# Moving GpSimd's two-input operations beside a gated recurrence to VectorE, in a hybrid decoder layer

## The chip, the core and the metric

The kernel runs on one core of one Trainium2 chip. The metric is the device time of one launch in microseconds (us), the median of the runs. The engines are named as in the profile: PE is TensorE (PEld its weight loads), DVE is VectorE, ACT is ScalarE, POOL is GpSimd, and SP is the queue that issues most transfers.

## What is computed

One layer of a decoder over 1024 positions of width 1024, in float32:

```python
proj = x @ w_in                      # [q | f | i | gate] of 4 x 512, attention q | k | v of 3 x 512
o_rec = hgrn2(q, f, i, gate)         # 4 heads of 128: S_t = diag(f_t) S_{t-1} + k_t^T i_t, o_t = S_t^T q_t
o_att = dilated_attention(aq, ak, av)  # 8 heads of 64, three window patterns
y = concat(o_rec, o_att) @ w_out
x = layer_norm(alpha * x + y)
x = layer_norm(alpha * x + relu(x @ w1)**2 @ w2)
```

In the recurrence q is silu(q), f = lb + (1 - lb) * sigmoid(f), k = 1 - f, and the output of each head is normalised, multiplied by a norm weight and by sigmoid(gate).

## The kernel before, in words

Products keep float32 accuracy by splitting an operand into a high part (a rounding copy on ACT) and a low part (raw minus high), and taking three matmuls: high*high, high*low and low*high.

The projection is cut into 22 weight tiles (`W_TILES`, lines 147 to 150). Fourteen of them (`NT1`) are run beside the recurrence: for each of two head groups v, two f, two q and g, then two tiles of attention v. The other eight (`LATE_TILES`) are run beside the attention. A tile is either natural (`natural_tile`, positions on the partitions, PSUM tile `nps`, eight steps of 24 matmuls) or transposed (`transposed_tile`, features on the partitions, PSUM tile `tps`, four steps of 24 matmuls). While tile n is computed, `w_conv` (line 170) splits the weights of tile n + 1 at step 2, and at step 4 if it has a second part: ACT copies the high part (L177), and POOL subtracts (L178). Tile 0 is split by DVE, in halves. Step 6 issues the load of tile n + 2 on SP. At the end of a g tile the sigmoid gates are multiplied by the norm weights, one 128x1024 product for each head, on POOL (L315).

The recurrence (`hgrn_group`, line 404) treats two heads at a time, as a tree over the sequence. `q` and `k` hold one head each as 128 features by 1024 positions; `tot` holds the decays. First the diagonal blocks are multiplied on PE (PSUM tile `lev`, 128 small matmuls), DVE keeps their diagonal (L424), and q is multiplied by the decay, head 0 on DVE and head 1 on POOL (L426). Then there are seven levels, j = 0 to 6. At each one PE computes the blocks between neighbouring segments of 2^j positions (`lev`), and DVE merges them into `dg` under a mask (L433, j under 5). Then each head's second half-segments of q are multiplied by the total decay of the first (DVE, L466), the first half-segments of k by the total decay of the second (POOL, L465), and the totals of the next level are formed (DVE, L468, into `totx`). Each L465 or L466 covers 128x512 elements, a strided half of the tile. The products of a level need the q and k of the level before. After level 4 the blocks of `dg` are copied to `AT` (L447 on ACT, L449 on DVE). Behind the last level k is transposed (`knps`, L482), states are built (`kvps`) and outputs formed (`ops`, normalised through a power on POOL, L526, and multiplied by the gates at L529).

The two streams are interleaved by `merge` (line 65): each stream states the cost of its steps, and the recurrence runs ahead until it has spent 0.7 of the projection's cost. That is the order in which the program is traced. Outside the first tile the framework's scheduler then fixes each engine's order at compile time; it prefers what was traced earlier among what it takes to be ready. On the chip every engine runs its own list strictly in order.

In the profile a line can be a helper's: all plain matmuls are L126, and the PSUM tile tells which they are. The k of the recurrence appears as `f` in POOL's rows, because both tiles of an f weight tile get that name.

Of the kernel before, what the change touches and what calls it, by code (L numbers as in the profile page):

```python
# [14 lines left out]
ALU = mybir.AluOpType  # L15
AX = mybir.AxisListType

P = 128
# [21 lines left out]
LATE_TILES = 8  # L40
# [49 lines left out]
def hybrid_layer_kernel(ctx: ExitStack, tc: tile.TileContext, x, w_in, w_out,  # L90
# [3 lines left out]
    PE, DVE, ACT, POOL, SP = nc.tensor, nc.vector, nc.scalar, nc.gpsimd, nc.sync  # L94
# [15 lines left out]
    def G(nm, dt=F32, shape=None):  # L110
        uid[0] += 1
        return gpool.tile(shape or [P, 1024], dt, name=f"{nm}_{uid[0]}", tag="g", bufs=50)
# [7 lines left out]
    def PS(tag, nm, shape=None):  # L120

        uid[0] += 1
        return ppool.tile(shape or [P, 512], F32, name=f"{nm}_{uid[0]}", tag=tag, bufs=PS_BUFS[tag])

    def mm(o, lhsT, rhs, start, stop, more=False):
        PE.matmul(o, lhsT, rhs, start=start, stop=stop, skip_group_check=more)  # L126

    def f32(ap):
        return ap.bitcast(F32)
# [17 lines left out]
    W_TILES = []  # L147
# [3 lines left out]
    W_COL = {"v": HI, "f": HF, "q": HQ, "g": HG, "av": AV, "aq": AQ, "ak": AK}  # L151
    NATURAL = ("v", "g", "av")
    wraw, whl = {}, {}

    def w_load(n, pieces=1):

        kind, g = W_TILES[n]
        nat = kind in NATURAL
        cw, kn = (256, 4) if nat else (128, 8)
        c0 = W_COL[kind] + cw * g  # L160
        wraw[n] = []
        for i in range(ND // kn):
            t = G("wraw", shape=[P, kn, cw])
            kp = kn // pieces
            for j in range(pieces):
                k0 = kn * i + kp * j
                SP.dma_start(t[:, kp * j:kp * (j + 1)], w_in[k0 * P:(k0 + kp) * P, c0:c0 + cw].rearrange("(k p) c -> p k c", p=P))
            wraw[n].append(t)

    def w_conv(n, i, engs=None):  # L170
        engs = engs or (POOL,)
        raw = wraw[n][i]
        hi, lo = G("whi", F32R, list(raw.shape)), G("wlo", F32R, list(raw.shape))
        kp = raw.shape[1] // len(engs)
        for j, eng in enumerate(engs):
            ks = slice(kp * j, kp * (j + 1))
            ACT.copy(hi[:, ks], raw[:, ks])  # L177
            eng.tensor_tensor(lo[:, ks], raw[:, ks], f32(hi[:, ks]), ALU.subtract)  # L178
        whl.setdefault(n, []).append((hi, lo))
# [10 lines left out]
    nrmw = cpool.tile([P, 512], F32, name="nrmw")  # L190
# [37 lines left out]
    def at_(tiles, kt, c0, n):  # L228
        return tiles[kt // 2][c0 // 512][:, kt % 2, c0 % 512:c0 % 512 + n]
# [41 lines left out]
    def natural_tile(n, kind, g, conv):  # L271

        if kind == "av":
            dst = [G("vs", F32R, [P, 8, P]) for _ in range(4)]
        else:
            dst = [G(kind, shape=[P, 8, P]) for _ in range(2)]
        for duo in range(4):
            ps = PS("s", "nps", [P, 2, 256])
            for i in range(2):
                sb = 2 * duo + i  # L280
                hooks = x_prep.get(sb, ()) if n == 0 else ()
                prods = [(kt, z, y) for kt in range(ND) for z, y in ((0, 0), (0, 1), (1, 0))]
                if n == 0 and sb == 0:
                    prods.sort(key=lambda v: v[2])
                for i_, (kt, z, y) in enumerate(prods):
                    if hooks and i_ % (24 // len(hooks)) == 0:
                        hooks[i_ * len(hooks) // 24]()
                    mm(ps[:, i, :], at_(xT["hl"[z]], kt, sb * P, P), whl[n][kt // 4][y][:, kt % 4, :],
                       i_ == 0, i_ == len(prods) - 1)
                conv(sb)  # L290
                yield 2600.0
            qs = slice(2 * duo, 2 * duo + 2)
            if kind == "av":
                for h in range(4):
                    i_ = ps[:, :, h * 64:(h + 1) * 64]
                    ACT.copy(dst[h][:, qs, 0:64], i_)
                    DVE.tensor_tensor(dst[h][:, qs, 64:128], i_, f32(dst[h][:, qs, 0:64]), ALU.subtract)
            else:
                for h in range(2):
                    i_ = ps[:, :, h * P:(h + 1) * P]  # L300
                    if kind == "g":
                        ACT.activation(dst[h][:, qs, :], i_, AF.Sigmoid)
                    else:
                        ACT.copy(dst[h][:, qs, :], i_)
        if kind == "av":
            if g == 0:
                at["v", 0], at["v", 1] = dst[0:2], dst[2:4]
            else:
                for h in range(4):
                    ACT.dma_start(v_d[h], f32(dst[h]).rearrange("p c v -> p (c v)"))  # L310
        else:
            for h in range(2):
                if kind == "g":
                    hh = 2 * g + h
                    POOL.tensor_tensor(dst[h], dst[h], nrmw[:, None, hh * P:(hh + 1) * P].to_broadcast([P, 8, P]), ALU.mult)  # L315
                    hd["gate", hh] = dst[h]
                else:
                    hd["v", 2 * g + h] = dst[h]
# [54 lines left out]
    def stage1_main(n0, n1):  # L373
# [4 lines left out]
        for n in range(n0, n1):  # L378
            kind, g = W_TILES[n]
            if n == 1:  # L380
                lower_bound()
            if n == NT1 - 2:
                SP.dma_start(bias, cf_d[:, C_BIAS:])
# [20 lines left out]
    def hgrn_group(g):  # L404
# [3 lines left out]
        q = [hd.pop(("q", h)) for h in heads]  # L408
        k = [hd.pop(("k", h)) for h in heads]
        tot = [hd.pop(("f", h)) for h in heads]  # L410
# [12 lines left out]
        blocks32(ps)  # L423
        DVE.tensor_tensor(dg, ps, dmask[:, None, :].to_broadcast([P, 16, 32]), ALU.mult)  # L424
        for i in range(2):
            (DVE if i == 0 else POOL).tensor_tensor(q[i], q[i], tot[i], ALU.mult)  # L426
        yield 3400.0
        for j in range(7):
            w = 1 << j
            if j < NLEV:  # L430
                ps = PS("t", "lev", [P, 16, 32])
                blocks32(ps)
                DVE.copy_predicated(dg, lmask[:, None, 32 * j:32 * j + 32].to_broadcast([P, 16, 32]), ps)  # L433
                cost = 3400.0
            elif j == 5:
                ps = PS("t", "lev", [P, 16, 32])
                for u in range(16):
                    kk, qq, c0 = k[u // 8], q[u // 8], (u % 8) * P
                    for b in (0, 64):
                        mm(ps[b:b + 32, u, :], kk[:, c0 + b:c0 + b + 32], qq[:, c0 + b + 32:c0 + b + 64], True, True)  # L440
                for i in range(2):
                    for b in (0, 64):
                        ACT.copy(AT[i][b:b + 32, :, b + 32:b + 64], ps[b:b + 32, 8 * i:8 * i + 8, :])
                    for b in range(4):
                        o = AT[i][32 * b:32 * b + 32, :, 32 * b:32 * b + 32]
                        if b % 2:
                            ACT.copy(o, dg[32 * b:32 * b + 32, 8 * i:8 * i + 8, :])  # L447
                        else:
                            DVE.tensor_copy(o, dg[32 * b:32 * b + 32, 8 * i:8 * i + 8, :])  # L449
                cost = 1800.0  # L450
            else:
                for i in range(2):
                    ps = PS("t", "lev", [64, 8, 64])
                    for c in range(8):
                        mm(ps[:, c, :], k[i][:, c * P:c * P + 64], q[i][:, c * P + 64:c * P + P], True, True)
                    ACT.copy(AT[i][0:64, :, 64:128], ps)
                cost = 1000.0

            n = S // (2 * w)
            for i in range(2):  # L460
                tv = tot[i].rearrange("p (n two) -> p n two", two=2) if j == 0 else \
                    totx[i][:, tofs:tofs + 2 * n].rearrange("p (n two) -> p n two", two=2)
                qv = q[i].rearrange("p (n two w) -> p n two w", two=2, w=w)[:, :, 1, :]
                kv = k[i].rearrange("p (n two w) -> p n two w", two=2, w=w)[:, :, 0, :]
                POOL.tensor_tensor(kv, kv, tv[:, :, 1:2].to_broadcast([P, n, w]), ALU.mult)  # L465
                DVE.tensor_tensor(qv, qv, tv[:, :, 0:1].to_broadcast([P, n, w]), ALU.mult)  # L466
                nofs = 0 if j == 0 else tofs + 2 * n
                DVE.tensor_tensor(totx[i][:, nofs:nofs + n], tv[:, :, 0], tv[:, :, 1], ALU.mult)  # L468
            tofs = 0 if j == 0 else tofs + 2 * n
            yield cost  # L470
# [63 lines left out]
        o_back(*pend)  # L534
        yield 450.0

    NT1 = len(W_TILES) - LATE_TILES
    bias, zt = G("bias"), G("zt", F32R, [P, 2, 2, 256])
    with tc.manual_schedule():
        for _ in stage1_main(0, 1):  # L540
            pass
    merge(stage1_main(1, NT1), flat(hgrn_group(0), hgrn_group(1)), R1)
    AT = None
# [212 lines left out]
    def filler():  # L756
        tail = stage1_main(NT1, len(W_TILES))

# [535 lines left out]
```

## Time and profile before

| what | value |
|---|---|
| median of three runs | 1264.65 us (1263.89 to 1265.03) |
| the profiled execution, its own time | 1261.03 us |
| its span, first to last instruction | 1259.2 us |
| PE busy | 1206.3 us (96%) |
| DVE busy | 809.8 us (64%) |
| ACT busy | 550.3 us (44%) |
| POOL busy | 303.7 us (24%) |
| mean granted TensorE clock | 0.991 |

A row of busy time counts how long an engine had an instruction in execution. Overlapping neighbours are pipelined, so that in the timeline the start of the next can lie before the end of the last. An instruction that waits for something while it is already counted as started is long in these rows. The granted clock is a share of the full 2.4 GHz; 0.5 is 1.2 GHz.

### The profile page before, as it was taken

How to read it: one execution, taken by the hardware profiler on the slowest of the kernel's cores; microseconds unless marked ns; L12 is line 12 of the kernel's file. 1: busy time of each engine (PE TensorE's matmuls, PEld its weight loads, DVE VectorE, ACT ScalarE, POOL GpSimd, SP SyncE). 2: the span in 40 equal slices, each digit the busy share in tenths (PEclk: the TensorE clock that was granted, in tenths of full speed). 3: DMA queues.
4: the chain of work that ended last, by engine and by line, in shares of the span. 5: the costliest groups of instructions: out<-in, count | busy, mean ns of one | idle time of the engine just before them, and what ended most of it. 6: DMA issues, size and time to landing. Idle time of an engine off the chain costs nothing.

```text
span 1259.2 us, 19842 instructions
## 1 busy us (share of the span) xinstructions
PE 1206.3 (96%) x7888; PEld 1024.8 (81%) x7888; DVE 809.8 (64%) x1302; ACT 550.3 (44%) x955; POOL 303.7 (24%) x231
## 2 busy tenths in 40 slices
PE   7998999899999989999999999999998999999996
PEld 7888988899787777887778888788886888888885
DVE  4035424562475664777796676766558798978788
ACT  5221342033576573654785554545555343334410
POOL 3236344633323333324200000000013132223100
PEclk9999999899999999999999999999999999999999
DMA  9000040003012576012215657566497636354312
GB/s 300 19 15 19 18 152 17 20 2 129 22 35 84 185 255 247 18 50 85 117 47 179 210 183 232 193 203 199 139 349 272 234 101 223 111 179 140 116 67 101
DMA packets 112765, 165.83 MB, mean 132 GB/s; under 512 B 8736, under 2 KB 64288, under 8 KB 112672
## 3 DMA queue, kind: packets, MB, share of 16 engines
q1 hardware_dynamic: 108400, 153.75, 36.3%
q10 hardware_dynamic: 4272, 10.82, 2.2%
q8 instruction: 62, 1.02, 0.3%
q14 instruction: 31, 0.25, 0.1%
HBM read 112.11 MB, written 52.43 MB: 131 GB/s over the span
## 4 chain that ended last, share of the span: by engine, by line
PE 77%; DVE 10%; DMA 4%; POOL 3%; issue 3%; ACT 3%; SPq 1%; DVEq 0%; POOLq 0%; ACTq 0%
PE f2ps L126 23%; PE tps L126 13%; PE nps L126 10%; PE fX L126 10%; PE pps L126 5%; PE fZ L126 5%; PE avps L126 3%; PE sps L126 2%; PE trps L630 2%; DVE tot L468 2%; PE fY L126 2%; DMA x<-x_d 2%; PE lev L126 1%; DVE w1l L817 1%; PE ops L126 1%
## 5 line engine op out<-in xcount | busy, mean ns | idle before, releaser
L817 POOL TENSOR_TENSOR h2l<-h2r,h2h 128x1024 fp32r<-128x1024 f32 x24 | 69.4, 2902 | 481.2 <-ACT h2h L816 444.3
L126 PE MATMUL f2ps<-w2l,h2h 128*128 128x512 f32 x448 | 174.5, 390 | 5.0 <-DVE w2l L817 5.0
L126 PE MATMUL f2ps<-w2h,h2l 128*128 128x512 f32 x448 | 174.0, 389 | 0.0
L126 PE MATMUL f2ps<-w2h,h2h 128*128 128x512 f32 x448 | 173.5, 389 | 0.5 <-ACT w2h L816 0.5
L126 PE MATMUL nps<-whi,xTh 128*128 128x256 f32 x384 | 113.9, 297 | 2.2 <-ACT whi L177 2.2
L126 PE MATMUL nps<-whi,xTl 128*128 128x256 f32 x384 | 110.2, 287 | 0.0
L126 PE MATMUL nps<-wlo,xTh 128*128 128x256 f32 x384 | 108.5, 285 | 0.0
L126 PEld LDWEIGHTS f2ps<-w2l,h2h 128*128 128x128 f32 x448 | 84.1, 188 | 23.8 <-DVE w2l L817 6.2
L126 PE MATMUL pps<-wo,oTs 128*128 128x512 f32 x384 | 100.8, 401 | 2.5 <-POOL wo L718 1.4
L126 PE MATMUL fX<-xh,w1h 128*128 128x512 f32 x256 | 100.0, 393 | 2.4 <-ACT hB L946 2.4
L126 PE MATMUL tps<-xTh,whi 128*128 128x512 f32 x256 | 101.8, 398 | 0.0
L126 PE MATMUL fX<-xl,w1h 128*128 128x512 f32 x256 | 100.0, 391 | 1.8 <-DVE xl L889 1.8
L126 PE MATMUL tps<-xTh,wlo 128*128 128x512 f32 x256 | 100.4, 392 | 0.0
L126 PE MATMUL tps<-xTl,whi 128*128 128x512 f32 x256 | 100.3, 392 | 0.0
L126 PE MATMUL fX<-xh,w1l 128*128 128x512 f32 x256 | 99.3, 390 | 0.0
L126 PEld LDWEIGHTS f2ps<-w2h,h2h 128*128 128x128 f32 x448 | 84.0, 188 | 18.2 <-ACT w2h L816 0.9
L126 PEld LDWEIGHTS f2ps<-w2h,h2l 128*128 128x128 f32 x448 | 84.1, 188 | 17.4
L1203 DVE TENSOR_TENSOR r<-r,f2ps 128x512 f32<-128x512 f32 x96 | 64.8, 680 | 30.1 <-PE f2ps L126 29.9
L126 PEld LDWEIGHTS pps<-wo,oTs 128*128 128x128 f32 x384 | 70.1, 190 | 17.4 <-POOL wo L718 2.9
L178 POOL TENSOR_TENSOR wlo<-wraw,whi 128x1024 fp32r<-128x1024 f32 x26 | 62.6, 2409 | 82.7 <-ACT whi L177 68.9
L612 POOL TENSOR_SCALAR pr<-pr,rec 128x896 f32<-128x896 f32 (+3 forms) x64 | 47.7, 748 | 140.4 <-DVE rec L611 119.9
L816 ACT CAST h2h<-h2r 128x1024 fp32r<-128x1024 f32 x56 | 58.8, 1050 | 44.3 <-PE f2ps L126 28.7
(205 smaller groups left out, 2733.7 us busy)
## 6 DMA issues: line engine op xcount, KB each, us to landing
h2r<-h_d SPq DMA_DIRECT2D x56, 512.0 KB, 4.8
w2r<-in_w_ff_dram SPq DMA_DIRECT2D x32, 512.0 KB, 5.8
wraw<-in_w_in_dram SPq DMA_DIRECT2D x26, 512.0 KB, 4.5
w1c<-in_w_ff_dram SPq DMA_DIRECT2D x32, 256.0 KB, 4.4
h_d<-hA SPq DMA_DIRECT2D x16, 512.0 KB, 3.7
h_d<-hC SPq DMA_DIRECT2D x16, 512.0 KB, 3.2
h_d<-hB SPq DMA_DIRECT2D x16, 512.0 KB, 4.4
att<-qk_d SPq DMA_DIRECT2D x12, 512.0 KB, 5.7
```

Of the source, the lines that this page charges most:

```text
L126: PE.matmul(o, lhsT, rhs, start=start, stop=stop, skip_group_check=more)
L178: eng.tensor_tensor(lo[:, ks], raw[:, ks], f32(hi[:, ks]), ALU.subtract)
L468: DVE.tensor_tensor(totx[i][:, nofs:nofs + n], tv[:, :, 0], tv[:, :, 1], ALU.mult)
L612: POOL.tensor_scalar(pr[:, 0:n], pr[:, 0:n], rec, 1.0, ALU.mult, ALU.mult)
L630: PE.transpose(ps[:, jj, tb, :], prs[tb][:, (j + jj) * P:(j + jj + 1) * P], ident)
L816: ACT.copy(hi, raw)
L817: eng.tensor_tensor(lo, raw, f32(hi), ALU.subtract)
L1203: DVE.tensor_tensor(rv, rv, ps, ALU.add)
```

## The change

The 18 low-part subtractions of weight tiles 1 to 13 (L178), the four gate products (L315), the first decay product of the second head (L426) and the 28 key decays (L465) are issued on DVE. At each level the key decay now stands behind the query decay of the same head and ahead of the totals. The subtractions of tile 14 and later stay on POOL, and so do the scaling of k (L344), the power of L526 and the memsets.

```diff
+    NT1 = len(W_TILES) - LATE_TILES
...
     def w_conv(n, i, engs=None):
-        engs = engs or (POOL,)
+        engs = engs or ((DVE,) if n < NT1 else (POOL,))
...
                 if kind == "g":
                     hh = 2 * g + h
-                    POOL.tensor_tensor(dst[h], dst[h], nrmw[:, None, hh * P:(hh + 1) * P].to_broadcast([P, 8, P]), ALU.mult)
+                    DVE.tensor_tensor(dst[h], dst[h], nrmw[:, None, hh * P:(hh + 1) * P].to_broadcast([P, 8, P]), ALU.mult)
...
         for i in range(2):
-            (DVE if i == 0 else POOL).tensor_tensor(q[i], q[i], tot[i], ALU.mult)
+            DVE.tensor_tensor(q[i], q[i], tot[i], ALU.mult)
...
-                POOL.tensor_tensor(kv, kv, tv[:, :, 1:2].to_broadcast([P, n, w]), ALU.mult)
                 DVE.tensor_tensor(qv, qv, tv[:, :, 0:1].to_broadcast([P, n, w]), ALU.mult)
+                DVE.tensor_tensor(kv, kv, tv[:, :, 1:2].to_broadcast([P, n, w]), ALU.mult)
```

## Rows read from the trace of the kernel before

**Rows 1.** The page's part 1: PE's busy time over the whole span.

```profile
PE 1206.3 (96%) x7888; PEld 1024.8 (81%) x7888; DVE 809.8 (64%) x1302; ACT 550.3 (44%) x955; POOL 303.7 (24%) x231
```

**Rows 2.** Stretches: us, busy time and count of each engine, PEclk, DMA share, GB/s.

```profile
82.00:155.00 73.00, 67.54 (x1310) 65.21 (x1309) 40.43 (x54) 15.03 (x34) 36.16 (x20) 0.98 0.06 17
155.00:205.00 50.00, 50.00 (x253) 42.15 (x252) 10.85 (x27) 17.56 (x52) 19.08 (x13) 1.00 0.33 106
205.00:310.00 105.00, 99.87 (x1568) 97.15 (x1567) 55.92 (x102) 29.02 (x94) 48.57 (x30) 0.97 0.10 32
```

**Rows 3.** PE's waits over the span: us in total, times, longest.

```profile
PE lev L126 <- DVE q L466: 7.3, 2, 3.6
...
PE knps L482 <- POOL f L465: 2.2, 4, 0.8
...
PE lev L126 <- POOL f L465: 0.7, 2, 0.4
```

**Rows 4.** Stretches around PE's two long waits, columns as in rows 2.

```profile
97.40:101.00 3.60, 0.05 (x1) 0.00 (x0) 3.60 (x11) 0.66 (x2) 1.88 (x1) 1.00 0.00 0
101.00:105.00 4.00, 3.79 (x138) 3.65 (x139) 3.41 (x5) 0.00 (x0) 2.68 (x2) 0.57 0.46 135
221.00:226.00 5.00, 1.52 (x97) 1.45 (x101) 4.93 (x13) 0.40 (x2) 2.84 (x3) 0.79 0.02 3
226.00:234.00 8.00, 8.00 (x95) 7.94 (x86) 2.61 (x3) 0.00 (x0) 2.58 (x2) 0.70 0.01 2
```

**Rows 5.** Timeline of DVE, 84 to 104 us: start, us, operation.

```profile
86.66 1.23 DVE L426 TENSOR_TENSOR q<-q,f 128x1024 f32<-128x1024 f32 x1 [2.24 <-PE lev L126]
...
88.41 2.90 DVE L468 TENSOR_TENSOR tot<-f 128x512 f32<-128x512 f32 x2
91.23 9.10 DVE L468 TENSOR_TENSOR tot<-tot 128x256 f32<-128x256 f32 x12
100.25 0.69 DVE L466 TENSOR_TENSOR q<-q,f 128x512 f32<-128x512 f32 x1
100.85 0.73 DVE L433 COPY_PREDICATED dg<-lmask,lev 128x512 f32<-128x512 int32 x1
```

**Rows 6.** Timeline of POOL, 84 to 104 us.

```profile
87.27 2.88 POOL L426 TENSOR_TENSOR q<-q,f 128x1024 f32<-128x1024 f32 x1 [5.61 <-PE lev L126]
91.09 1.61 POOL L465 TENSOR_TENSOR f<-f,f 128x512 f32<-128x512 f32 x1 [0.95 <-PE lev L126]
...
96.87 2.40 POOL L178 TENSOR_TENSOR wlo<-wraw,whi 128x1024 fp32r<-128x1024 f32 x1
```

**Rows 7.** Groups by form, 0 to 320 us: count, busy us, mean ns, idle before.

```profile
L178 POOL TENSOR_TENSOR wlo<-wraw,whi 128x1024 fp32r<-128x1024 f32 x20 | 48.2, 2412 | 56.4 <-ACT whi L177 42.6 <-issue 13.0 <-DVE q L466 0.6
L465 POOL TENSOR_TENSOR f<-f,tot 128x512 f32<-128x512 f32 x24 | 33.7, 1420 | 23.1 <-PE lev L126 23.0 <-POOL f L465 0.2
L466 DVE TENSOR_TENSOR q<-q,tot 128x512 f32<-128x512 f32 x24 | 30.4, 1272 | 27.6 <-PE lev L126 27.4
L468 DVE TENSOR_TENSOR tot<-tot 128x256 f32<-128x256 f32 x4 | 8.6, 2184 | 0.0
L466 DVE TENSOR_TENSOR q<-q,f 128x512 f32<-128x512 f32 x4 | 2.7, 682 | 0.0
L426 DVE TENSOR_TENSOR q<-q,f 128x1024 f32<-128x1024 f32 x2 | 2.5, 1225 | 4.5 <-PE lev L126 4.5
L468 DVE TENSOR_TENSOR tot<-tot 128x64 f32<-128x64 f32 x4 | 0.7, 214 | 0.0
```

**Rows 8.** Timeline of ACT, 84 to 104 us: the high parts of two weight pieces.

```profile
90.83 2.00 ACT L177 CAST whi<-wraw 128x1024 fp32r<-128x1024 f32 x2
```

**Rows 9.** The chain that ended last: PE's projection between two levels.

```profile
111.12 5.94 PE nps L126 x48
```

**Rows 10.** Timeline of PE near 456 us.

```profile
456.03 0.58 PE L126 MATMUL avps<-pth,vs 128*128 128x256 f32 x1 [2.14 <-DVE opair L688]
```

**Rows 11.** The stretch around that wait, columns as in rows 2.

```profile
455.00:460.00 5.00, 3.97 (x14) 3.47 (x15) 3.62 (x9) 3.46 (x7) 2.53 (x2) 0.66 0.79 313
```

More of the change, by code (lines that the diff above doesn't have):

```diff
@@ L535, in hgrn_group @@
         yield 450.0
-    NT1 = len(W_TILES) - LATE_TILES
     bias, zt = G("bias"), G("zt", F32R, [P, 2, 2, 256])
```

## The prediction
> **What bounds the kernel now.** The page's busy times come first: PE is busy 96% of the span, so only time in which PE idles or is clocked down can be won [rows 1]. The stretches then show where the change can act. In the two in which a head group's recurrence runs PE idles 5.5 us of 73 and 5.1 us of 105, and the granted clock is below 1; between them PE has no gap at all [rows 2]. PE's waits name the idle time: 7.3 us in two waits of the level products for a query decay on DVE, 0.7 us in two for a key decay on POOL, and 2.2 us in four, where the transposes of k wait for the last key decay on POOL [rows 3]. That is 10.2 of the 10.6 us. Last, the short stretches around the two long waits show what follows each: the clock falls to its lower level, 1.2 GHz, as PE comes back from an idle of 3.6 us. What this costs is the share of the clock withheld while PE worked: 4.00 x 0.43 = 1.7 us in the first group, and 1.52 x 0.5 + 8.00 x 0.30 = 3.2 us in the second, 4.9 us together [rows 4].
>
> Why was DVE late? Between 88.41 and 100.25 it ran nothing but the 14 products of the totals, ahead of the first query decay [rows 5]. They are not that long: the 128x64 form takes 0.21 us, but the 128x256 form 2.18 us, ten times as much for four times the data [rows 7]. Over those same microseconds POOL ran two-input operations almost without a pause: one of 2.88 us from 87.27, then four back to back until 99.27, where the last one, begun at 96.87, ends [rows 6]. DVE's next decay begins 1 us later. I read that as exclusion: a DVE operation with two SBUF inputs stands still while POOL has a two-input one in execution. The query decays carry the same mark: 0.682 us on average at level 0, 1.272 us at the other levels, for the same 128x512 [rows 7].
>
> **The parts, one by one.**
>
> *Key decays.* 28 operations leave POOL, where they took 1.42 us or more, and join DVE. The price on DVE is that of the query decay of the same shape and stride, 0.68 us, and DVE's next operation starts 0.60 behind such a one (100.25, 100.85) [rows 5, 7]. A plain level is then four decays and one masked copy, 5 x 0.61 = 3.1 us, in the cover of 48 projection matmuls of 5.94 us [rows 9]. If that cover were gone, 3.1 us would lie on the path at each of 14 levels.
>
> *Weight low parts, gate products, first decay of head 1.* 18 + 4 + 2 operations of 128x1024 at DVE's 1.225 us in place of 2.41 us for the low parts [rows 7]: 2 x 1.2 of them in the first two levels of a group, two gate products in one later level, one or two low parts in another. Such a level costs 3.1 + 2.5 = 5.6 us at most, still under 5.94, with little to spare. Low parts outside the recurrence lie beside stretches in which DVE is busy 10.85 of 50 us [rows 2], and cost nothing. The SP loads issued behind them wait for the same buffers, free a little earlier.
>
> *The first level, which decides.* From 86.66 DVE runs two first decays, 2.45 us, and the diagonal, 0.6: 89.7. The totals without a blocker are, for each head, 0.68 (the price of 128x512), about 0.42 and 0.28 (estimates between 0.68 and 0.21 by size), 0.21, and three shorter ones of about 0.17, 2.1 us in all: two heads end at 93.9. Then head 0's two decays to 95.1; one low part to 96.3, whose high part is ready from 91.8 [rows 8]; the masked copy to 96.9; head 1's decays to 98.1. PE comes free at 97.4, needs head 0 first and head 1 some 0.65 us later, at 98.1. So the wait falls from 3.6 us to nothing, or to 1.2 if both low parts are queued ahead of head 1. Bounds for each group: 0 (best order) and 3.6 (as now); more only if the long forms are DVE's own price, a rival below. I take 0.3, nearest to the order in which POOL's own rows place the two low parts around a decay [rows 6].
>
> *Waits that shrink a little.* The 0.7 us behind POOL's key decays goes, since no 2.4 us operation of POOL stands ahead of them. Of the 2.2 us before the transposes I let 0.3 us go: two serial decays of 0.6 take the place of one of 1.42.
>
> *Waits that are added.* Behind a low part on DVE's strictly ordered list stand the decays of a level, and for those waits PE. If its high part is late, all wait. Bounds: 0, as all covers above suffice, and 0.3 + 2.45 us at each of the levels with three 1.2 us operations. I take 1.1 us over both groups. What is late next is DVE itself in the level with the gates.
>
> *The clock.* No idle of 3.6 us, no fall: 4.9 us back. How short a gap must be for that, the trace doesn't say sharply: near 456 us a wait of 2.14 us was also followed by a stretch at 0.66 [rows 10, 11], while the waits of up to 0.8 us in rows 3 were not.
>
> *The sum.* 7.3 - 0.6 = 6.7, plus 4.9, 0.7 and 0.3, less 1.1: 11.5 us. Against the profiled execution's own 1261.03 that gives 1249.5. That execution stands 3.6 us below the median of the runs, and I take the same difference for the changed kernel: 1264.65 - 11.5 = 1253.2 us. Beyond 310 us nothing is changed, and PE is the bound, so an earlier start should carry through to the end.
>
> **The rivals.**
>
> *Half of it.* DVE's list may put both low parts, or the totals of later levels, between level 0's products and head 1's decays. A wait of 2.3 us then stays in each group, and the clock still falls, as it did behind 2.14 us [rows 10, 11]. The gain is 2 x 1.3 + 0.7 + 0.3 = 3.6 us: 1261.0. For it: the low parts do fall just there [rows 6]. Against: the totals alone give back more than 7 us.
>
> *Absorbed.* The first 310 us end earlier, but the attention's order or its transfers give it back: 1264 us, within 0.2% of before. For it: a scheduler that sees other engine loads may order later work otherwise. Against: nothing in that part waits for a fixed point in time.
>
> *Slower: DVE is the bound by itself.* The long rows could be DVE's own price for strided and short accesses, and not POOL's doing. Then a level costs 4 x 1.27 + 0.61 = 5.7 us, a low part in it makes 6.9 (1.0 over the cover), two gate products 8.2 (2.2 over): about 4.2 a group. The totals keep their 11.8 us and the first wait grows by the decay, the key decays and the low part that now precede, some 2.5 us. Together 2 x 6.7 = 13.4 us: about 1278. It decides from 5.94 us a level on. Against: level 0's decays, stride two as well, take 0.682 [rows 7].
>
> The spacing itself is shown: 0.60 us from the start of an operation of 0.69 to the next [rows 5]. The Trainium skill (VectorE: DVE Perf Modes, sections "The DRAIN you can't avoid" and "Rules for kernel authors") speaks against this change: behind each operation it puts a flush of about the duration less 266 ns, unless the next one may start earlier, and asks for few operations. By that flush a plain level would cost about 5.6 us, one with a low part 7.8 and one with two gates 10, the first wait would be about 6.6, and the sum would be an estimated 18 us slower than before; the trace shows no such gap, so it gets no chance beyond this rival's.
>
> **How the numbers follow.** The forecast has 0.75, half of it 0.13, absorbed 0.07, slower 0.05. The forecast's own range is 1249.5 (all 10.2 us and the 4.9 back) to 1258. The range reaches up to the half case, 1261, and leaves out the other two. A measurement of this kernel can tell about 0.2%, 2.5 us, from no change: the half case is still faster by that. So faster 0.86, same 0.08, slower 0.06.
>
> **What would show it right or wrong.** Right: DVE's totals of 128x256 near 0.4 us and its decays near 0.7; PE's wait for L466 under 1 us each; granted clock 1.00 from 82 to 310; that stretch shorter by about 11 us, and all behind it unchanged. Wrong: the long forms stay long with POOL idle (exclusion is not the cause); or they shrink and PE still waits, now for DVE behind a low part or a gate; or the stretch shrinks and the attention grows.

## The result and the profile after

The changed kernel takes 1249.29 us (median of five runs, 1248.10 to 1250.61) against 1263.89 us for the kernel before on the same chip (1261.03 to 1265.03): a ratio of 0.989, 95% interval 0.9878 to 0.9903, 14.6 us faster. Between the two profiled executions it is 12.9 us, 1261.03 to 1248.10.

The stretches of the changed kernel, with the columns of [rows 2] and [rows 4]:

```profile
82.00:155.00 73.00, 73.00 (x1352) 70.25 (x1351) 39.75 (x80) 18.37 (x52) 1.68 (x2) 1.00 0.06 17
205.00:310.00 105.00, 105.00 (x1467) 100.60 (x1467) 53.17 (x128) 35.15 (x105) 12.82 (x9) 1.00 0.15 52
97.40:101.00 3.60, 3.60 (x148) 3.43 (x147) 3.53 (x14) 0.66 (x2) 0.00 (x0) 1.00 0.02 5
101.00:105.00 4.00, 4.00 (x35) 3.94 (x33) 0.79 (x2) 0.00 (x0) 0.00 (x0) 1.00 0.02 4
```

PE has no gap left beside the recurrence and works at the full clock throughout; none of the three waits of [rows 3] exists any more. The last high-part projection matmul of tile `nps` begins at 294.1 us instead of 309.3. So 15.2 us were won there, and the next stage, the attention, starts earlier by the same 15.2 (first `sps` at 319.0 instead of 334.2). The high-part matmuls of `nps`, before and after (count, shortest, median and longest in ns, first and last start in us):

```profile
L126 PE MATMUL nps<-whi,xTh x384: 277/283/583, 8.3 to 309.3; 128*128 128x256 f32 x192
```

```profile
L126 PE MATMUL nps<-whi,xTh x384: 277/283/582, 8.3 to 294.1; 128*128 128x256 f32 x192
```

The groups of DVE between 0 and 320 us, by form (L466, L467, L469, L179 and L450 are L466, L465, L468, L178 and L449 before):

```profile
L179 DVE TENSOR_TENSOR wlo<-wraw,whi 128x1024 fp32r<-128x1024 f32 x18 | 21.7, 1222 | 7.1 <-ACT whi L178 7.1
L466 DVE TENSOR_TENSOR q<-q,tot 128x512 f32<-128x512 f32 x24 | 16.4, 684 | 14.4 <-PE lev L126 14.2
L467 DVE TENSOR_TENSOR f<-f,tot 128x512 f32<-128x512 f32 x24 | 16.4, 683 | 0.0
...
L467 DVE TENSOR_TENSOR f<-f,f 128x512 f32<-128x512 f32 x4 | 2.7, 684 | 0.0
...
L450 DVE COPY AT<-dg 32x256 f32<-32x256 f32 x8 | 2.2, 280 | 0.1
L469 DVE TENSOR_TENSOR tot<-tot 128x256 f32<-128x256 f32 x4 | 1.5, 424 | 0.0
```

Against [rows 7] the query decays fall from 1.272 to 0.684 us and the 128x256 totals from 2.184 to 0.424. DVE has 52 instructions more, but its busy time in the two stretches falls slightly, from 96.3 to 92.9 us [rows 2], though the second stretch now ends 15 us further into what follows. Over the whole span it rises by 6.0 us, to 815.8; at 0.684 us for a decay and 1.222 for a 128x1024 operation the 52 would add an estimated 48.

The timeline of DVE around the first level, start and duration in us:

```profile
88.89 1.22 DVE L427 TENSOR_TENSOR q<-q,f 128x1024 f32<-128x1024 f32 x1
90.02 1.29 DVE L469 TENSOR_TENSOR tot<-f 128x512 f32<-128x512 f32 x2
91.23 0.97 DVE L469 TENSOR_TENSOR tot<-tot 128x256 f32<-128x256 f32 x3
92.11 0.68 DVE L466 TENSOR_TENSOR q<-q,f 128x512 f32<-128x512 f32 x1
...
94.54 0.68 DVE L467 TENSOR_TENSOR f<-f,f 128x512 f32<-128x512 f32 x1
95.14 2.35 DVE L179 TENSOR_TENSOR wlo<-wraw,whi 128x1024 fp32r<-128x1024 f32 x2
97.41 1.19 DVE L469 TENSOR_TENSOR tot<-tot 128x128 f32<-128x128 f32 x9
```

Two things differ from [rows 5], not one. No operation is long, and **DVE's list has another order**: only 5 of the 14 totals stand ahead of the decays of level 0; the other 9 have moved behind them. Nobody wrote that into the change. It is the compile-time scheduler's answer to the change, and the experiments had to tell the two apart.

### The profile page after: what moved, and what is told of

The parts are those of the page before. It is cut to its first block, busy times and chain, and to the rows that moved or that the text cites. A ratio compares the mean times of both kernels' runs of the same rounds, so it can differ in the third digit from the quotient of the medians.

```text
span 1246.3 us, 19786 instructions
## 1 busy us (share of the span) xinstructions
PE 1203.6 (97%) x7888; PEld 1022.3 (82%) x7888; DVE 815.8 (65%) x1354; ACT 550.3 (44%) x955; POOL 204.9 (16%) x179
## 4 chain that ended last, share of the span: by engine, by line
PE 81%; DVE 7%; DMA 4%; ACT 3%; issue 3%; POOL 2%; SPq 1%; DVEq 0%; POOLq 0%; ACTq 0%
PE f2ps L126 23%; PE tps L126 13%; PE nps L126 11%; PE fX L126 10%; PE pps L126 5%; PE fZ L126 5%; PE avps L126 3%; PE sps L126 2%; PE trps L630 2%; DMA x<-x_d 2%; PE fY L126 2%; PE lev L126 2%; PE ops L126 1%; DVE w1l L817 1%; DMA qk_d<-ak 1%
## 5 line engine op out<-in xcount | busy, mean ns | idle before, releaser
L126 PEld LDWEIGHTS nps<-whi,xTh 128*128 128x128 f32 x384 | 74.6, 194 | 3.2 <-ACT whi L178 2.4
L126 PEld LDWEIGHTS nps<-whi,xTl 128*128 128x128 f32 x384 | 74.5, 194 | 0.0
```

## The experiments

The table gives medians, ratios to the kernel before on the same chip, and PE's idle time in the stretches 82 to 155 and 205 to 310 us together (10.6 us before, from [rows 2]). In all of these kernels the granted clock of both stretches is 1.00.

| kernel | us | ratio, 95% interval | PE idle, us |
|---|---|---|---|
| changed kernel | 1249.29 | 0.989 (0.9878 to 0.9903) | 0 |
| decays only | 1250.80 | 0.9911 (0.9892 to 0.993) | 2.7 |
| low parts and gates only | 1251.31 | 0.9906 (0.9889 to 0.9923) | 4.5 |
| changed, spare two-input work | 1251.24 | 0.9913 (0.9892 to 0.9933) | 2.5 |
| changed, spare memsets | 1250.05 | 0.9886 (0.9859 to 0.9914) | 0 |
| 4 low parts only | 1254.53 | 0.9927 (0.9908 to 0.9945) | 5.0 |
| 2 first decays only | 1252.37 | 0.9916 (0.989 to 0.9941) | 3.6 |
| before, totals behind | 1251.28 | 0.9915 (0.99 to 0.9931) | 3.0 |
| changed, totals ahead | 1249.96 | 0.9897 (0.9882 to 0.9911) | 0 |

### Does GpSimd's work hold VectorE, wanted or not?

Three kernels add work to GpSimd that nobody reads. All other engines' lists are those of the changed kernel. Spare two-input products:

```diff
+    scr = cpool.tile([P, 384], F32, name="scr")
+    def spare(h):
+        for c in (0, 320, 640):
+            POOL.tensor_tensor(scr, h[:, c:c + 384], h[:, c:c + 384], ALU.mult)
...
+        if 0 < n < NT1:
+            spare(f32(hi).rearrange("p k c -> p (k c)"))
```

> The changed kernel, and beside each low part of tiles 1 to 13 GpSimd also computes three two-input products of 128x384 from the high part into a scratch tile that nothing reads, as soon as the high part is there. The lists of all other engines are the same. Theory (holding): VectorE's totals, decays and copies in these stretches grow to over 1 us on average though they wait for no result, PE's waits before level 1 come back with 1.5 to 4 us in each group: 1254 to 1262 us. Rival (late results of GpSimd): nobody waits for GpSimd, so the time is that of the changed kernel, 1249 to 1250 us.

In the second kernel a copy of one element per partition and three memsets stand in place of the products:

```diff
...
+        POOL.tensor_copy(scr[:, 0:1], h[:, 0:1])
...
+            POOL.memset(scr, 0.0)
...
```

> As the kernel with spare products, but in place of each three products stand a copy of one element a partition (it makes GpSimd start at the same time) and three memsets of 128x384, which read no SBUF. Theory (holding by operations that read two inputs): VectorE's operations stay at their prices, 0.68 us for 128x512, 1249 to 1251 us. If any activity of GpSimd that writes SBUF holds VectorE: operations beside it grow by up to 1 us and the time goes to 1251 to 1255 us. Rival (late results): 1249 to 1250 us.

In the third, a scaling:

```diff
...
+            POOL.tensor_scalar(scr, h[:, c:c + 384], 1.0, 1.0, ALU.mult, ALU.mult)
...
```

> As the kernel with spare two-input products, but with one-input operations (a scaling) of 128x384. Theory (GpSimd holds VectorE for as long as it reads SBUF, with one input as well): VectorE's totals and low parts beside them grow, by less than with two inputs, since each lasts about half as long: 128x1024 low parts between 1.25 and 1.45 us on average. Rival (two inputs are needed): all of VectorE's operations keep their prices, as beside memsets.

The groups by form, 0 to 320 us, with the two-input products:

```profile
L185 DVE TENSOR_TENSOR wlo<-wraw,whi 128x1024 fp32r<-128x1024 f32 x18 | 26.1, 1463 | 7.1 <-ACT whi L184 7.1
...
L475 DVE TENSOR_TENSOR f<-f,f 128x512 f32<-128x512 f32 x4 | 4.0, 1002 | 0.0
...
L477 DVE TENSOR_TENSOR tot<-tot 128x128 f32<-128x128 f32 x4 | 2.4, 599 | 0.0
...
L175 POOL TENSOR_TENSOR scr<-whi 128x384 f32<-128x384 f32 x54 | 65.3, 1209 | 108.1 <-ACT whi L184 105.1
```

With the memsets:

```profile
L186 DVE TENSOR_TENSOR wlo<-wraw,whi 128x1024 fp32r<-128x1024 f32 x18 | 21.9, 1231 | 7.0 <-ACT whi L185 7.0
...
L476 DVE TENSOR_TENSOR f<-f,f 128x512 f32<-128x512 f32 x4 | 2.8, 694 | 0.0
...
L176 POOL MEMSET scr<- 128x384 f32 x54 | 22.8, 423 | 3.1
L174 POOL COPY scr<-whi 128x1 f32<-128x1 f32 x18 | 21.5, 1194 | 116.0 <-ACT whi L185 115.8
```

The memsets do run beside decays, as the timelines of POOL and of DVE show:

```profile
93.57 1.38 POOL L176 MEMSET scr<- 128x384 f32 x3
```

```profile
94.00 0.69 DVE L475 TENSOR_TENSOR q<-q,f 128x512 f32<-128x512 f32 x1
94.60 0.69 DVE L476 TENSOR_TENSOR f<-f,f 128x512 f32<-128x512 f32 x1
```

With the scalings:

```profile
L185 DVE TENSOR_TENSOR wlo<-wraw,whi 128x1024 fp32r<-128x1024 f32 x18 | 23.6, 1322 | 7.0 <-ACT whi L184 7.0
...
L475 DVE TENSOR_TENSOR f<-f,f 128x512 f32<-128x512 f32 x4 | 3.3, 834 | 0.0
...
L175 POOL TENSOR_SCALAR scr<-whi 128x384 f32<-128x384 f32 x54 | 47.8, 884 | 118.5 <-ACT whi L184 115.2
```

Work of which nobody awaits a result stretches DVE's low parts from 1.222 to 1.463 us and the first key decays from 0.684 to 1.002. Scalings do it too (1.322 and 0.834), memsets don't (1.231 and 0.694). The kernel with scalings was run once, 1249.07 us. So the holding is real, and of the three kinds of spare work only the two that read SBUF hold. It is mutual: the copy of one element per partition takes GpSimd 1.19 us beside DVE's low parts. But the time was forecast too high: with the products PE's waits came back with 2.5 us in all, 1251.24 us, with an interval that overlaps that of the changed kernel. None of them stands before level 1, where they were expected: 1.7 us lie at later levels of the second group, 0.8 before its transposes. By the time alone, theory and rival aren't told apart here; the rows of DVE do that. Holding VectorE need not cost PE anything.

The Trainium skill (SBUF — State Buffer, section "SBUF: two separate sides") says that the two engines share one pair of ports under an exclusive lock, held for a whole instruction, and that a VectorE operation with two SBUF inputs contends only with GpSimd operations that read SBUF. The rows above agree on what holds: 1.002 and 0.834 beside reading work, 0.694 beside memsets. That a hold lasts a whole instruction is not read from them.

### Which part of the change was needed?

Decays on VectorE, the rest back on GpSimd:

```diff
-        engs = engs or ((DVE,) if n < NT1 else (POOL,))
+        engs = engs or (POOL,)
...
-                    DVE.tensor_tensor(dst[h], dst[h], nrmw[...], ALU.mult)
+                    POOL.tensor_tensor(dst[h], dst[h], nrmw[...], ALU.mult)
```

> Only the decays (28 key decays and the first decay of head 1) are on VectorE; the 18 low parts and four gate products are back on GpSimd. PE's order is that of the changed kernel, instruction for instruction. Theory (a two-input operation of GpSimd holds VectorE's operations on SBUF): the two low parts of 2.4 us that fall beside level 0 stop VectorE from about 92 to 97 us, so a wait of 1 to 3 us comes back before level 1 in each group, perhaps with a fall of the clock: about 1255 us, 1251 to 1259; 128x512 decays again above 0.8 us on average. Rival (what cost time was that the key decays came late from a slow engine, whoever ran beside): all key decays are as fast as in the changed kernel, no wait, 1249 to 1250 us.

The timelines of DVE and of POOL around level 0:

```profile
93.59 2.28 DVE L466 TENSOR_TENSOR q<-q,f 128x512 f32<-128x512 f32 x1
95.80 2.89 DVE L467 TENSOR_TENSOR f<-f,f 128x512 f32<-128x512 f32 x1
98.61 1.20 DVE L469 TENSOR_TENSOR tot<-tot 128x128 f32<-128x128 f32 x9
```

```profile
92.15 5.99 POOL L179 TENSOR_TENSOR wlo<-wraw,whi 128x1024 fp32r<-128x1024 f32 x2 [10.35 <-ACT whi L178]
```

The two low parts hold head 1's decays as expected, 2.28 and 2.89 us in place of 0.68. But PE waited only 0.5 us for them, since head 0's decays were through and 9 totals stood behind. 1250.8 us instead of the 1255 expected: the time lies between the theory's range and the rival's, and it is the long rows that speak for holding.

The reverse, low parts and gates on VectorE, the key decays and the first decay of head 1 back on GpSimd:

```diff
-            DVE.tensor_tensor(q[i], q[i], tot[i], ALU.mult)
+            (DVE if i == 0 else POOL).tensor_tensor(q[i], q[i], tot[i], ALU.mult)
...
-                DVE.tensor_tensor(kv, kv, tv[:, :, 1:2].to_broadcast([P, n, w]), ALU.mult)
+                POOL.tensor_tensor(kv, kv, tv[:, :, 1:2].to_broadcast([P, n, w]), ALU.mult)
```

> Only the low parts and the gate products are on VectorE; the key decays and the first decay of head 1 are back on GpSimd. Theory (holding): the first decay of 2.9 us and the key decays of level 0 still stop the totals, some 4 to 5 us of holding beside level 0 in place of 11: a wait of 0.5 to 2 us before level 1, and the four waits before the transposes of k back with about 2 us: 1253 us, 1250 to 1257. Rival (late key decays): nearly the whole difference to the kernel before stays, 1259 to 1264 us.

PE's waits, 30 to 310 us (us in total, times, longest):

```profile
PE knps L483 <- POOL f L467: 2.6, 4, 0.8
PE lev L126 <- DVE q L466: 1.8, 2, 0.9
```

1251.31 us: the key decays on the slow engine are not what cost the time. Here all 14 totals still stand ahead of the decays, and 0.9 us of wait is left in each group. Either half of the change gives most of the whole, so the parts don't add up. The next two kernels start from the kernel before and move very little.

Four of the 52 operations, the low parts that fall beside level 0 and 1:

```diff
-        engs = engs or (POOL,)
+        engs = engs or ((DVE,) if n in (6, 12) else (POOL,))
```

> The kernel before with only 4 of the 52 operations moved to VectorE: the low parts of the two weight tiles (6 and 12) that are split beside levels 0 and 1 of each group. PE's order is that of the kernel before. Theory (GpSimd holds VectorE, and it costs time only where the held work outlasts PE's projection beside it, which is the case before level 1 alone): without these 4.8 us of holding in each group the wait before level 1 falls from 3.6 to about 1 us, the clock doesn't fall, and some 9 to 11 of the 13 to 15 us come back: 1251 to 1255 us. The waits before the transposes of k stay at about 2 us. Rival (each held operation costs its share, so 4 of 52 give little): a wait over 2.5 us stays, 1257 to 1263 us.

Two of the 52, the first decays of head 1:

```diff
-            (DVE if i == 0 else POOL).tensor_tensor(q[i], q[i], tot[i], ALU.mult)
+            DVE.tensor_tensor(q[i], q[i], tot[i], ALU.mult)
```

> The kernel before with only 2 of the 52 operations moved: the first decay of the second head, once in each group. Theory (holding, and the totals as what is held): from 91 to 99 us GpSimd's key decays and low parts still follow each other without a pause, so the totals finish where they did, the wait before level 1 stays at 2.5 to 3.7 us and the clock falls: 1259 to 1264 us. Rival (the first operation of the chain sets all behind it): the wait shrinks by the 1.6 us that this decay gets faster, to 2 us, and the clock may hold: 1253 to 1259 us.

Four low parts: 1254.53 us, and the wait before level 1 falls to 0.9 us in each group, as expected; all 14 totals still stand ahead. Two first decays: 1252.37 us, against the 1259 to 1264 that my theory wanted and the 1253 to 1259 of its rival. The wait that was to stay is gone but for 0.2 us. The timeline of DVE in that kernel shows why:

```profile
92.13 0.70 DVE L466 TENSOR_TENSOR q<-q,f 128x512 f32<-128x512 f32 x1
...
93.70 1.42 DVE L466 TENSOR_TENSOR q<-q,f 128x512 f32<-128x512 f32 x1
95.04 8.93 DVE L468 TENSOR_TENSOR tot<-tot 128x64 f32<-128x64 f32 x7
```

GpSimd still holds the totals, 8.93 us for seven of them. But they are other totals: the scheduler has put the decays ahead of them, so nobody waits. The theory as it stood, holding alone, fell here; the order of the list had to be part of it.

What turns the order can be read off all the kernels. Where the first decay of head 1 stays on GpSimd (the kernel before, low parts and gates only, 4 low parts only), 14 totals stand ahead of level 0's decays; where it is on VectorE and no edge fixes the order (the changed kernel, decays only, spare work, 2 first decays, the two steps further), 5 do. So one operation in each group goes with the new order. Why the scheduler answers to it, no run shows.

### Order and holding, one without the other

The kernel before with an ordering edge (`issue_after`) that puts each level's totals behind both heads' query decays; no operation changes its engine:

```diff
-                nofs = 0 if j == 0 else tofs + 2 * n
-                DVE.tensor_tensor(totx[i][:, nofs:nofs + n], tv[:, :, 0], tv[:, :, 1], ALU.mult)
+                last = nc.cur_bb.bb.instructions[-1]
+            with tc.issue_after(last):
+                for i in range(2):
...
+                    DVE.tensor_tensor(totx[i][:, nofs:nofs + n], tv[:, :, 0], tv[:, :, 1], ALU.mult)
```

> The kernel before, every operation on its old engine, with one thing changed: on VectorE's list the totals of a level stand behind the query decays of both heads (an ordering edge, no wait). PE's, ScalarE's and SP's lists are those of the kernel before. Theory now (the loss comes from both together: GpSimd holds VectorE, and the list puts all 14 totals, which nobody needs yet, ahead of the decays that PE waits for): the wait before level 1 falls below 1 us and the clock holds, though GpSimd's work and its holding stay: 1250 to 1255 us. Rival (holding alone is the cause, the order is of no account): 1258 to 1264 us.

DVE's timeline and, below it, the groups by form and PE's waits:

```profile
91.25 0.69 DVE L466 TENSOR_TENSOR q<-q,f 128x512 f32<-128x512 f32 x1 [2.49 <-PE lev L126]
...
92.52 1.37 DVE L466 TENSOR_TENSOR q<-q,f 128x512 f32<-128x512 f32 x1
93.81 4.81 DVE L473 TENSOR_TENSOR tot<-f 128x512 f32<-128x512 f32 x2
```

```profile
L466 DVE TENSOR_TENSOR q<-q,tot 128x512 f32<-128x512 f32 x24 | 30.3, 1271 | 12.5 <-PE lev L126 12.5
L473 DVE TENSOR_TENSOR tot<-f 128x512 f32<-128x512 f32 x4 | 9.6, 2443 | 0.0
```

```profile
PE knps L487 <- POOL f L465: 2.2, 4, 0.8
PE lev L126 <- POOL f L465: 0.7, 2, 0.4
```

The holding is all there, query decays 1.271 us as before and totals even longer, and yet the two waits of 3.6 us and the slow clock behind them are gone: 1251.28 us without moving a single operation. GpSimd's list followed in one point: in each group the key decay of head 1 now stands ahead of both low parts. That belongs to this result, too, but it can't be what freed PE: the two long waits were for a query decay [rows 3], and in the kernel before that key decay had ended by 96.9 us, when POOL's second low part began [rows 6], before PE came free at 97.4.

The opposite corner, the changed kernel with all totals ahead:

```diff
+        for j in range(7):
+            for i in range(2):
...
+                DVE.tensor_tensor(totx[i][:, nofs:nofs + n], tv[:, :, 0], tv[:, :, 1], ALU.mult)
+        last = nc.cur_bb.bb.instructions[-1]
...
+                with tc.issue_after(last):
+                    DVE.tensor_tensor(qv, qv, tv[:, :, 0:1].to_broadcast([P, n, w]), ALU.mult)
+                    DVE.tensor_tensor(kv, kv, tv[:, :, 1:2].to_broadcast([P, n, w]), ALU.mult)
```

> The changed kernel, every operation on its new engine, with all 14 totals ahead of level 0's decays on VectorE's list, as in the kernel before; both low parts come to stand ahead of them too. PE's list is that of the changed kernel. Theory now (order costs only as much as the operations ahead take, and without holding they take their own prices): totals 4.2 us and low parts 2.4 us end about 1 us too late for PE, a wait of 0.5 to 1.5 us in each group and no fall of the clock: 1250 to 1253 us. Rival (the order is the cause, holding of no account): the wait of 3.6 us is back: 1258 to 1264 us.

```profile
90.92 1.53 DVE L435 TENSOR_TENSOR tot<-tot 128x256 f32<-128x256 f32 x7
92.37 1.22 DVE L179 TENSOR_TENSOR wlo<-wraw,whi 128x1024 fp32r<-128x1024 f32 x1
...
95.69 0.68 DVE L477 TENSOR_TENSOR q<-q,f 128x512 f32<-128x512 f32 x1
...
97.49 0.69 DVE L478 TENSOR_TENSOR f<-f,f 128x512 f32<-128x512 f32 x1
```

Here every total and both low parts stand ahead of the decays, and PE doesn't wait at all: 1249.96 us, with an interval that overlaps that of the changed kernel. It is a little better than the wait of about 1 us that I expected, and it is close: PE begins level 1 with head 0 at 97.6 us and needs head 1 an estimated 0.65 later, while head 1's last decay ends at 98.2. PE's own list is the same in all four kernels up to the last level, 48 projection matmuls ahead of level 1 each time, so a different cover isn't the reason. **The loss needs both**: totals ahead of the decays, and GpSimd holding them. The change takes away both, and either would have been nearly enough.

### Two steps further

The same cure in other stages: the attention's scaling of probabilities and late low parts (first kernel), the low parts of the second MLP product (second), both (third).

```diff
-        engs = engs or ((DVE,) if n < NT1 else (POOL,))
+        engs = engs or (DVE,)
...
-        POOL.tensor_scalar(pr[:, 0:n], pr[:, 0:n], rec, 1.0, ALU.mult, ALU.mult)
+        DVE.tensor_scalar(pr[:, 0:n], pr[:, 0:n], rec, 1.0, ALU.mult, ALU.mult)
```

> A step further than the change: the low parts of the eight late weight tiles and the scaling of the attention's probabilities (64 one-input operations) are also on VectorE. Theory (holding costs only where VectorE's work is not covered): the attention's waits for VectorE (3.8, 3.0 and 1.7 us) are partly held work, but 64 scalings at about 0.5 us join a VectorE that is 66% busy there, and they stand on the way to the transposes: 1244 to 1254 us, about the changed kernel. Rival (the less on GpSimd, the faster, everywhere): 1240 to 1245 us.

```diff
-            hs = hi_lo(h, POOL if k in (1, 3, 5) else DVE, "h2", FF2S)
+            hs = hi_lo(h, DVE, "h2", FF2S)
```

> A step further in another place: the 24 low parts of the second MLP product's activations (2.9 us each on GpSimd) are also on VectorE. Theory (holding costs only what isn't covered): VectorE is 80 to 90% busy there, gets 24 x 1.22 = 29 us more and loses the holding, which is under 24 x 2.9 = 70 us: the waits of 3.3 us for its low parts may go, or grow: 1243 to 1256 us. Rival (the less on GpSimd, the faster): 1240 to 1246 us; opposite rival (VectorE becomes the bound of this stage): 1256 to 1270 us.

> The changed kernel with the attention's scalings and late low parts and the MLP's low parts on VectorE as well, the two further steps together. If they add up: 1243.9 less 1.3, 1241 to 1244 us. If the attention's step gains nothing by itself: 1243 to 1245 us.

The attention's step gives 1248.01 us (a ratio of 0.9879, 0.9862 to 0.9896), not to be told from the changed kernel, as expected. The MLP's gives **1243.88 us, a ratio of 0.9845 (0.983 to 0.986)** to the kernel before, and is faster than the changed kernel and the attention's step; it lies in the ranges of both the theory and its first rival and doesn't separate them. Its groups between 910 and 1240 us:

```profile
L817 DVE TENSOR_TENSOR h2l<-h2r,h2h 128x1024 fp32r<-128x1024 f32 x56 | 68.3, 1219 | 4.7 <-ACT h2h L816 4.6
...
L817 DVE TENSOR_TENSOR w2l<-w2r,w2h 128x1024 fp32r<-128x1024 f32 x38 | 46.3, 1219 | 0.5 <-ACT w2h L816 0.5
```

The same rows in the changed kernel, where 24 activation low parts are POOL's:

```profile
L817 DVE TENSOR_TENSOR w2l<-w2r,w2h 128x1024 fp32r<-128x1024 f32 x38 | 61.0, 1607 | 6.2 <-ACT w2h L816 5.6 <-PE f2ps L126 0.5
...
L817 DVE TENSOR_TENSOR h2l<-h2r,h2h 128x1024 fp32r<-128x1024 f32 x31 | 44.1, 1424 | 1.2 <-ACT h2h L816 1.1
```

So DVE takes 24 more operations and its busy time in this stretch still falls, from 277.3 to 274.0 us; PE's wait for the low parts goes from 3.3 to 1.5 us. That is 1.8 of the 5.4 us by which the `f2ps` stage is shorter between the two profiled executions (312.2 against 317.6). The changed kernel's has two falls of the clock there that this one lacks, but such falls come and go: the stage has none in the kernel before and in the one with spare products, one with spare memsets. So how much of this gain is the clock and how much the moved work isn't shown, though its four single runs lie close together (1243.19 to 1244.19). Both steps together give 1246.80 us (a ratio of 0.9861, 0.9837 to 0.9884), more than expected and no better than the MLP's alone, with single runs from 1241.64 to 1247.97; why is open.

## Why the prediction was right, and where its sizes were off

The forecast was 1253.2 us, a gain of 11.5; measured are 1249.29 and 14.6. So the time lies 0.2 us below 1249.5, the end of the forecast's own range at which everything counted comes back. The main path was right, and the sizes erred to one side.

**The bound and the two long waits** were read rightly: 7.3 us of waits and 4.9 us of slow clock went, whole.

**The cause** was read half. "Exclusion" is shown by the spare work. But the prediction's first level kept the old order, all totals ahead of the decays, and gave the whole cure to the shorter durations. The kernel with totals ahead is nearly that chain, with both low parts ahead of the decays: head 1's last decay ends at 98.2, where 98.1 was worked out with one low part and a wait of 1.2 us with both, and PE doesn't wait. What the changed kernel did was easier: decays ahead of 9 totals, head 1 ready at 95.2. The rivals knew the list only as a danger (low parts ahead of decays); that it could move in favour was missed.

**The terms.** The remaining 0.6 us of long waits was 0, and the 1.1 us of added waits was 0: a level with two gates still fitted into its cover. "Of the 2.2 us before the transposes I let 0.3 us go": all 2.2 went. PE's list changed there, too: four projection matmuls now stand ahead of a group's first transposes, and six instead of two ahead of the next. The kernel with two first decays keeps PE's old list and the 2.2 us, but also GpSimd's key decays; no run has one without the other, so what each gave is not shown. Together, 0.6 + 1.1 + 1.9 = 3.6 us, these are nearly all of what lies between the sum, 11.5 us, and the 15.2 us measured at the end of the projection.

**The reference.** The sum took the changed kernel's median to stand 3.6 us above its profiled execution, as before; it stands 1.2 above. That is 2.4 of the 3.9 us between 1253.2 and 1249.29. The rest is the 3.7 us more that were won, less 2.3 lost after the projection.

**"An earlier start should carry through to the end"**: nearly. 15.2 us at the end of the projection are 12.9 at the end of the profiled execution. The last `f2ps` stage, from the first to the last matmul of high parts, takes 317.6 us instead of 316.1, with two falls of the clock near 935 and 952 us, of which these stretches show the granted clock, third from the end, at 0.66 and 0.71:

```profile
935.00:940.00 5.00, 5.00 (x17) 3.93 (x16) 1.35 (x3) 2.62 (x3) 0.00 (x0) 0.66 0.94 368
...
950.00:955.00 5.00, 3.87 (x12) 2.71 (x11) 5.00 (x4) 5.00 (x6) 2.52 (x1) 0.71 1.02 407
```

No run here says why the clock falls there; the single runs of one kernel differ by as much (1248.10 to 1250.61).

**The rivals.** Half of it and absorbed didn't happen. DVE as the bound by itself is refuted by the same instructions at 0.684 us beside an idle GpSimd. So is the flush behind each operation as a price: in the changed kernel the operation of 1.22 us that starts at 88.89 is followed by the next one 1.13 us after that start.

## What to carry to other kernels

A long row on VectorE beside a busy GpSimd may be a wait in disguise: compare it with the same shape where GpSimd is idle, before you take it for a price. Then look at what stands ahead of the critical operation on the same list; a held operation costs time only if somebody waits behind it, so an ordering edge can be worth nearly as much as moving fifty operations (11.4 against 14.6 us here). And a change of engines changes a planner's order as well: compare the lists of both kernels before you credit the engines.

## What the runs showed of the hardware that was not expected

- The holding goes both ways: a copy of one element per partition took GpSimd 1.19 us on average beside VectorE's low parts of 1.23 us (spare memsets), against 0.19 us for a copy of 128x4 at the start of the same kernel.
- One-input copies of VectorE from SBUF are held, too: 1.026 us before (median 0.672, longest 2.458), 0.280 after. The masked copy, whose second input lies in PSUM, isn't: 0.737 before and 0.734 after.
- The profile counts the held time as busy time of the held engine, so in the two stretches DVE's busy time fell from 96.3 to 92.9 us although it got more operations, and over the whole span 52 more cost it 6.0 us.
